# A decoder layer on one core: gates, branch projections and first FFN projection with tokens stationary, results turned over

## The chip, the core and the metric

The kernel runs on one core of a Trainium2 chip. TensorE multiplies a stationary operand, loaded into its array by a weight load, with a moving operand; VectorE and ScalarE do the elementwise work, GpSimd a little, and SyncE's queue (SP) issues the loads. The metric is the device time of one execution in microseconds, the median of several runs. A profile of one execution gives the rows that are shown below; in it PE is TensorE's matmul, PEld its weight load, DVE VectorE, ACT ScalarE, POOL GpSimd and SPq the SyncE queue.

## What is computed

One layer of a hybrid decoder for 256 tokens of width 2048, in float32. Cut to what matters here:

```python
h = modulate(rms_norm(x, norm1_g), sh1, sc1)
u, lru_gate, q, k, v, mix_gates = split(h @ w_in + b_in)
y_lru = rg_lru(causal_depthwise_conv(u)) * gelu(lru_gate)
y_attn = sliding_window_attention(q, k, v, sinks)
gate_lru, gate_attn = split(sigmoid(mix_gates))
merged = gate_lru * (y_lru @ w_lru_out) + gate_attn * (y_attn @ w_attn_out)
x = x + g1 * (merged @ w_o)
h2 = modulate(rms_norm(x, norm2_g), sh2, sc2)
gate, up = split(h2 @ w_ffn_in)
x = x + g2 * ((silu(gate) * up) @ w_ffn_out)
return rms_norm(x, final_g)
```

`w_in` has 22 slabs of 512 columns (the last eight are the mixer gates), each branch projection and `w_o` four, `w_ffn_in` 22 (eleven of gate, eleven of up), and `w_ffn_out` has 44 k-tiles of 2048 columns.

## The kernel before

**Split products.** Every float32 operand is split into a high part (a copy to fp32r by ScalarE, `do_hi`, L285) and a low part (the rest, by VectorE, `do_lo`, L297). A product is three: high x high, high x low, low x high, summed in PSUM (`mm3`, L327 to L329).

**Steps.** The weights come as items of 1024 columns: two k-tiles (128 rows of weights each) of a slab of 512 columns, 512 KB. `step(i)` (L308) issues loads six items ahead, high parts four and low parts three ahead, writes the products of item i into TensorE's order, and then lets other work in. What follows a slab's products (its *post*, a generator) advances by one stage at the start of each later step. Work that belongs to no slab (*sides*: the modulations, the RG-LRU, the attention) advances in stages at the end of a step, as far as a model of the engines' pace, which is part of the program, lets it in. All engines work in the order that this program writes; there is no other scheduler.

**Order of the layer.** The first projection's slabs for u, the GeLU gate, q, k, v (`wi`); the gates of the first branch (`wgl`, 4 slabs); the RG-LRU branch's projection (`wl`, 4); the gates of the second branch (`wga`, 4); the attention's projection (`wa`, 4); `wo` (4); the second norm; then for s in 0 to 10 a gate slab (`fg`) and an up slab (`fu`); the last projection (`pf`, `pl`).

**Three forms of product.** In `add_slab` (L331) the weights are stationary (128 columns of them) and the 256 tokens move: 12 products of 256 columns for a k-tile of a slab, and the result has features along the partitions. With `in_rows` the tokens are stationary (128 of them) and 512 weight columns move: 6 products of 512 columns, and the result has tokens along the partitions. Before, only the V slab (`wi` with SL_V) used `in_rows`. The last projection has a loop of its own with the same shape (L1093). The FFN's first projection uses `add_wide`: weights stationary, and the high and the low part of h2 side by side as 512 moving columns (L1000), then the low part of the weights with 256 columns (L1005): 8 products a k-tile, and two halves that are added afterwards (L1019, L1020). A slab thus has 192 products of 256 columns, or 96 of 512, or 64 of each.

**Posts that the change touches.** `gate_post` (L796): four sigmoids on ScalarE, with the bias as a value for each partition. `lru_post`, `att_post`: two multiplications by the gate on VectorE (L807, L815), the addition of both branches (L817), the split into `mh`, `ml` (L820, L823). `gate_f_post`, `up_f_post`: halves added, SiLU (L1027), multiplied (L1037), split into `fh`, `fl` (L1040, L1043). The results `mh`, `ml`, `fh`, `fl` must have features along the partitions: they are the operands of `wo` and of the last projection.

**PSUM.** Two pools of four banks: `ps_w` (two banks for a slab, so two slabs at a time; `fg` takes all four) and `ps_m` (side work; `fu` takes all four).

## Time and profile before

| | us |
|---|---|
| median of 3 runs (1611.21 to 1613.03) | 1611.26 |
| span of the profiled execution, first to last instruction | 1607.2 |
| TensorE busy | 1591.6 |
| VectorE busy | 1146.6 |
| ScalarE busy | 798.5 |

The profile covers one execution, from its first to its last instruction; the median lies 4.1 us above that span. TensorE's products are pipelined and their ends are modelled: a row's duration is longer than the distance to the next product's start, so rates are read from starts.

### The profile page before, as it was taken

To read this page: it belongs to the slowest core of one execution; us is meant where nothing else is said; L and a number is where in the kernel's file an instruction comes from. 1 tells how busy PE (TensorE), PEld (TensorE's weight loads), DVE (VectorE), ACT (ScalarE), POOL (GpSimd) and SP (SyncE) were. 2 spreads that over 40 slices of the span, in tenths; PEclk is the share of its full clock that TensorE was granted. 3 is DMA by queue.
4 is the path that set the end of the run, shared out by engine and by line. 5 is a ranking of instruction groups with operands and counts; after the bars stand their busy time and mean duration, and the time that the engine had idled before them with its cause. 6 is when DMAs were issued, how large, how long until landed. Compare 5 with 4: busy or idle time off the path is not lost.

```text
span 1607.2 us, 26845 instructions
## 1 busy us (share of the span) xinstructions
PE 1591.6 (99%) x10642; PEld 1460.8 (91%) x10642; DVE 1146.6 (71%) x1472; ACT 798.5 (50%) x1058; POOL 3.0 (0%) x9
## 2 busy tenths in 40 slices
PE   8999999999999999999999999999999999999998
PEld 6999999999999999999998888888888888888886
DVE  6889988989888878788557888455555555444465
ACT  4754444586854455444446444444444444333343
POOL 0000000000000000000000000000000000000000
PEclk9999999999999999999999999999999999999999
DMA  9999998766687878998756898666656566766663
GB/s 319 340 332 327 329 333 285 281 197 226 205 268 247 288 259 273 331 321 298 241 179 226 303 322 314 192 184 185 186 183 194 184 186 207 253 194 195 194 190 127
DMA packets 112596, 397.55 MB, mean 247 GB/s; under 512 B 12499, under 2 KB 13651, under 8 KB 112085
## 3 DMA queue, kind: packets, MB, share of 16 engines
q1 hardware_dynamic: 112470, 395.83, 73.6%
q8 instruction: 83, 1.36, 0.3%
q14 instruction: 43, 0.35, 0.1%
HBM read 391.59 MB, written 4.19 MB: 246 GB/s over the span
## 4 chain that ended last, share of the span: by engine, by line
PE 97%; DVE 1%; DMA 1%; ACT 1%; issue 0%; SPq 0%; ACTq 0%; DVEq 0%
PE pf L1093 11%; PE fu L1000 10%; PE fg L1000 10%; PE wi L329 6%; PE wi L328 6%; PE wi L327 6%; PE fg L1005 5%; PE fu L1005 5%; PE pl L1093 3%; PE wgl L327 2%; PE wo L328 2%; PE wo L327 2%; PE wa L329 2%; PE wa L328 2%; PE wa L327 2%; PE wo L329 2%
## 5 line engine op out<-in xcount | busy, mean ns | idle before, releaser
L285 ACT CAST hi<-raw 128x1024 fp32r<-128x1024 f32 (+1 forms) x552 | 565.0, 1027 | 733.3 <-PE pf L1093 108.0
L297 DVE TENSOR_TENSOR lo<-raw,hi 128x1024 fp32r<-128x1024 f32 (+1 forms) x552 | 655.6, 1192 | 361.8 <-PE pf L1093 92.8
L1000 PE MATMUL fg<-h_both,hi 128*128 128x512 f32 x704 | 250.5, 400 | 0.5 <-DVE h_both L952 0.5
L1000 PE MATMUL fu<-h_both,hi 128*128 128x512 f32 x704 | 249.8, 399 | 0.0
L327 PE MATMUL wi<-h_both,hi 128*128 128x256 f32 x784 | 222.6, 284 | 0.0
L329 PE MATMUL wi<-h_both,lo 128*128 128x256 f32 x784 | 222.1, 283 | 0.5 <-DVE lo L297 0.5
L328 PE MATMUL wi<-h_both,hi 128*128 128x256 f32 x784 | 221.9, 283 | 0.0
L1005 PE MATMUL fu<-h_both,lo 128*128 128x256 f32 x704 | 197.7, 281 | 0.0
L1005 PE MATMUL fg<-h_both,lo 128*128 128x256 f32 x704 | 197.7, 281 | 0.0
L1000 PEld LDWEIGHTS fg<-h_both,hi 128*128 128x128 f32 x704 | 132.3, 188 | 34.2 <-DVE h_both L952 0.7
L1000 PEld LDWEIGHTS fu<-h_both,hi 128*128 128x128 f32 x704 | 132.3, 188 | 33.5 <-ACT pa L588 0.3
L329 PEld LDWEIGHTS wi<-h_both,lo 128*128 128x128 f32 x784 | 150.4, 192 | 0.8 <-DVE lo L297 0.7
L328 PEld LDWEIGHTS wi<-h_both,hi 128*128 128x128 f32 x784 | 150.5, 192 | 0.2
L327 PEld LDWEIGHTS wi<-h_both,hi 128*128 128x128 f32 x784 | 150.4, 192 | 0.2
L1005 PEld LDWEIGHTS fg<-h_both,lo 128*128 128x128 f32 x704 | 133.0, 189 | 0.7 <-issue 0.7
L1005 PEld LDWEIGHTS fu<-h_both,lo 128*128 128x128 f32 x704 | 133.0, 189 | 0.2 <-issue 0.2
L414 DVE CUSTOM_DVE_ANT_0 aw<-aw,crow,modc 128x1024 f32<-128x1024 f32 x79 | 100.8, 1280 | 14.2 <-DMA aw<-in_ada_t_dram 14.0
L414 DVE CUSTOM_DVE_ANT_0 aw<-aw,crow,vec 128x1024 f32<-128x1024 f32 x79 | 100.9, 1280 | 4.9 <-DMA aw<-in_ada_t_dram 4.8
L1093 PE MATMUL pf<-lo,fh 128*128 128x512 f32 x264 | 88.5, 389 | 0.0
L1093 PE MATMUL pf<-hi,fh 128*128 128x512 f32 x264 | 88.4, 389 | 0.0
L1093 PE MATMUL pf<-hi,fl 128*128 128x512 f32 x264 | 88.4, 389 | 0.0
L327 PE MATMUL wl<-yh,hi 128*128 128x256 f32 x256 | 74.9, 293 | 0.0
(228 smaller groups left out, 2930.5 us busy)
## 6 DMA issues: line engine op xcount, KB each, us to landing
raw<-in_w_f_dram SPq DMA_DIRECT2D x176, 512.0 KB, 3.5
raw<-in_w_in_dram SPq DMA_DIRECT2D x160, 512.0 KB, 6.4
aw<-in_ada_t_dram SPq DMA_DIRECT2D x158, 512.0 KB, 5.6
raw<-in_w_f2a_dram SPq DMA_DIRECT2D x44, 512.0 KB, 4.2
raw<-in_w_lru_dram SPq DMA_DIRECT2D x32, 512.0 KB, 6.2
raw<-in_w_att_dram SPq DMA_DIRECT2D x32, 512.0 KB, 6.6
raw<-in_w_o_dram SPq DMA_DIRECT2D x32, 512.0 KB, 3.6
aw<-in_ada_g_dram SPq DMA_DIRECT2D x32, 512.0 KB, 5.2
```

Of the source, the lines that this page charges most:

```text
L285: nc.scalar.copy(hi[:, :cols], live[i][0][:, :cols])
L297: nc.vector.tensor_tensor(lo[:, :cols], raw[:, :cols], f32(hi[:, :cols]), op=ALU.subtract)
L327: nc.tensor.matmul(ps, lhsT=lh, rhs=rh, start=start, stop=False, skip_group_check=True)
L328: nc.tensor.matmul(ps, lhsT=lh, rhs=rl, start=False, stop=False, skip_group_check=True)
L329: nc.tensor.matmul(ps, lhsT=ll, rhs=rh, start=False, stop=stop, skip_group_check=True)
L414: nc.vector.tensor_tensor_reduce(out=r, in0=r, in1=crow[:, j * CH:(j + 1) * CH], op0=ALU.mult, op1=ALU.add, scale=1.0, scalar=dst if j els ...
L1000: nc.tensor.matmul(banks[f].rearrange("p j n -> p (j n)"), lhsT=hi[:, cs], rhs=h2["both"][:, kt, :, :].rearrange("p j n -> p (j n)"), star ...
L1005: nc.tensor.matmul(banks[f][:, 0, :], lhsT=lo[:, cs], rhs=h2["both"][:, kt, 0, :], start=False, stop=kt == NK - 1, skip_group_check=True,)
L1093: nc.tensor.matmul(fin[t, n], lhsT=l[:, rows(t)], rhs=w[:, c0:c0 + 512], start=kt == 0 and k == 0, stop=kt == (EARLY if (t, n) == (1, 3) e ...
```

## The change

The 16 slabs `wgl`, `wl`, `wga`, `wa` now go through `add_slab` with `in_rows`; so do the 22 slabs of the FFN's first projection, and `add_wide` is gone. Their results have tokens along the partitions. For the gates the bias is then a row: it is loaded into every partition (`load_gate_bias`, one load of 128x512 for each gate slab, issued at the slab's third step) and added by VectorE, and one sigmoid follows. The products with the gates stay as they were, on (2, 512) in place of (4, 256). The merged slabs and the FFN's hidden slabs are turned over by TensorE (`turned`: 8 transposes of 128x128 into two banks of `ps_m`), and split out of PSUM (`parts_of`). The attention's mask is made later, in the buffer of `rx`, to make room for the bias buffer.

```diff
+    def in_rows_of(bank):
+        return bank.rearrange("p j n -> p (j n)")
...
-    def add_slab(slab, name, act, k0, k1, post, in_rows=False, before=None):
+    def add_slab(slab, name, act, k0, k1, post, in_rows=False, before=None, late=0):
...
+                if a == k0 + late and before is not None:
+                    before()
                 if a == k0:
-                    if before is not None:
-                        before()
                     banks.extend(wtile(f"{name}_{k0}_{i}") for i in range(2))
...
         free(b4=4)
+        make_mask()
...
+    def load_gate_bias(s):
+        def before():
+            bias[s] = sp.tile([P, 512], F32, tag="bm", name=f"bm{s}", bufs=1)
+            nc.sync.dma_start(bias[s], bm_row[(s - SL_GL) * 512:(s - SL_GL + 1) * 512].partition_broadcast(P))
+        return before
+
     def gate_post(s, i, to):
         def post(banks):
-            dst = b4(f"gate{s}")
-            for f in range(4):
-                b = V_BIN + 4 * s + f
-                nc.scalar.activation(dst[:, f, :], banks[f // 2][:, f % 2, :], AF.Sigmoid, bias=vec[:, b:b + 1])
+            dst, b = b4(f"gate{s}", F32, (2, 512)), bias.pop(s)
+            for t in range(2):
+                nc.vector.tensor_tensor(dst[:, t, :], in_rows_of(banks[t]), b, op=ALU.add)
+            yield 1.4, 0
+            nc.scalar.activation(dst, dst, AF.Sigmoid)
             to[i] = dst
-            yield 0, 1.8
+            yield 0, 1.1
         return post
+
+    def gated(banks, g):
+        for t in range(2):
+            nc.vector.tensor_tensor(g[:, t, :], in_rows_of(banks[t]), g[:, t, :], op=ALU.mult)
...
+    def turned(rows_, name):
+
+        pts = [mtile(f"{name}{i}").rearrange("p (j n) -> p j n", n=S) for i in range(2)]
+        for j in range(4):
+            for t in range(2):
+                nc.tensor.transpose(pts[j // 2][:, j % 2, rows(t)], rows_[:, t, j * P:(j + 1) * P], ident)
+        return pts
+
+    def parts_of(pts, hi, lo):
+
+        for i in range(2):
+            nc.scalar.copy(hi[:, 2 * i:2 * i + 2, :], pts[i])
+        yield 0, 1.2
+        for i in range(2):
+            nc.vector.tensor_tensor(lo[:, 2 * i:2 * i + 2, :], pts[i], f32(hi[:, 2 * i:2 * i + 2, :]), op=ALU.subtract)
+        free(m=2)
+        yield 1.4, 0
 
     def att_post(s):
         def post(banks):
-            for i in range(2):
-                a2 = ga[s][:, 2 * i:2 * i + 2, :]
-                nc.vector.tensor_tensor(a2, banks[i], a2, op=ALU.mult)
-            yield 1.2, 0
+            gated(banks, ga[s])
+            yield 1.4, 0
             nc.vector.tensor_tensor(ga[s], ga[s], gl[s], op=ALU.add)
             yield 1.13, 0
-            mh = b4(f"mh{s}", F32R)
-            nc.scalar.copy(mh, ga[s])
-            yield 0, 0.95
-            ml = b4(f"ml{s}", F32R)
-            nc.vector.tensor_tensor(ml, ga[s], f32(mh), op=ALU.subtract)
+            pts = turned(ga[s], f"mt{s}")
+            yield 0, 0
+            mh, ml = b4(f"mh{s}", F32R), b4(f"ml{s}", F32R)
+            yield from parts_of(pts, mh, ml)
...
-        add_slab(w_lru[s], f"wl{s}", yact, 0, NK, lru_post(s))
+        add_slab(w_lru[s], f"wl{s}", yact, 0, NK, lru_post(s), True)
     for i in range(4):
-        add_slab(w_in[SL_GA + i], f"wga{i}", hact, 0, NK, gate_post(SL_GA + i, i, ga))
+        add_slab(w_in[SL_GA + i], f"wga{i}", hact, 0, NK, gate_post(SL_GA + i, i, ga), True, load_gate_bias(SL_GA + i), 4)
...
     def gate_f_post(s):
         def post(banks):
-            sg = silu[s] = b4(f"sg{s}")
-            yield from halves_added(banks, sg)
-            nc.scalar.activation(sg, sg, AF.Silu)
-            yield 0, 1.1
+            sg = silu[s] = b4(f"sg{s}", F32, (2, 512))
+            for t in range(2):
+                nc.scalar.activation(sg[:, t, :], in_rows_of(banks[t]), AF.Silu)
+            yield 0, 1.3
         return post
 
     def up_f_post(s):
         def post(banks):
             sg = silu.pop(s)
-            up = b4(f"up{s}")
-            yield from halves_added(banks, up)
-            free(m=4)
-            nc.vector.tensor_tensor(sg, up, sg, op=ALU.mult)
-            yield 1.13, 0
...
+            for t in range(2):
+                nc.vector.tensor_tensor(sg[:, t, :], in_rows_of(banks[t]), sg[:, t, :], op=ALU.mult)
+            yield 1.4, 0
+            pts = turned(sg, f"ft{s}_")
+            yield 0, 0
+            fh, fl = b4(f"fh{s}", F32R), b4(f"fl{s}", F32R)
+            yield from parts_of(pts, fh, fl)
...
-        add_wide(w_f1[s], f"fg{s}", True, gate_f_post(s))
-        add_wide(w_f1[11 + s], f"fu{s}", False, up_f_post(s))
+        add_slab(w_f1[s], f"fg{s}", h2act, 0, NK, gate_f_post(s), True)
+        add_slab(w_f1[11 + s], f"fu{s}", h2act, 0, NK, up_f_post(s), True)
```

How the rows of the engines move, at three places (the first name is what is written, behind the arrow what is read, then the size).

TensorE, the first k-tile of the second gate slab (`wgl` is the slab's bank, `h_both` the tokens, `hi` and `lo` the weights' parts), before:

```order
L329 MATMUL wgl_0_0_4561<-h_both,lo_4486 128x256
L327 MATMUL wgl_0_0_4561<-h_both,hi_4443 128x256
L328 MATMUL wgl_0_0_4561<-h_both,hi_4443 128x256
L329 MATMUL wgl_0_0_4561<-h_both,lo_4486 128x256
L327 MATMUL wgl_0_1_4562<-h_both,hi_4443 128x256
L328 MATMUL wgl_0_1_4562<-h_both,hi_4443 128x256
L329 MATMUL wgl_0_1_4562<-h_both,lo_4486 128x256
```

and now:

```order
L320 MATMUL wgl_0_0_4465<-lo_4416,h_both 128x512
L321 MATMUL wgl_0_0_4465<-hi_4385,h_both 128x512
L319 MATMUL wgl_0_1_4466<-hi_4385,h_both 128x512
L320 MATMUL wgl_0_1_4466<-lo_4416,h_both 128x512
L321 MATMUL wgl_0_1_4466<-hi_4385,h_both 128x512
```

The products with a low half of the weights stay in the middle of the k-tile; two rows of 256 columns become one of 512, and a bank now holds 128 tokens in place of 256 features.

VectorE, behind the first gate slab (`uc` is the convolution of the RG-LRU, `lo` the low halves of the weights, `yl` the branch's low part), before:

```order
L297 TENSOR_TENSOR lo_4486<-raw_4370,hi_4443 128x1024
L297 TENSOR_TENSOR lo_4516<-raw_4401,hi_4484 128x1024
...
L645 SCALAR_TENSOR_TENSOR uc_4432<-acc_585,vec,uc_4432 128x255
L297 TENSOR_TENSOR lo_4559<-raw_4441,hi_4514 128x1024
L701 TENSOR_TENSOR yl_4480<-uc_3376,yh_4479 128x1024
L297 TENSOR_TENSOR lo_4598<-raw_4482,hi_4557 128x1024
```

and now:

```order
L286 TENSOR_TENSOR lo_4416<-raw_4336,hi_4385 128x1024
L286 TENSOR_TENSOR lo_4434<-raw_4355,hi_4414 128x1024
...
L638 SCALAR_TENSOR_TENSOR uc_4374<-acc_577,vec,uc_4374 128x255
L812 TENSOR_TENSOR gate_4456<-wgl_0_0_4276,bm_4319 128x512
L812 TENSOR_TENSOR gate_4456<-wgl_0_1_4277,bm_4319 128x512
L286 TENSOR_TENSOR lo_4463<-raw_4383,hi_4432 128x1024
L286 TENSOR_TENSOR lo_4490<-raw_4412,hi_4461 128x1024
L694 TENSOR_TENSOR yl_4410<-uc_3376,yh_4409 128x1024
```

The two additions of the gates' bias stand ahead of the next low half, and the branch's low part moves one low half back.

TensorE, in the second FFN gate slab, where the first hidden slab (`sg`) is turned over (`ft`), now:

```order
L319 MATMUL fg_0_1_8941<-hi_8872,h_both 128x512
L320 MATMUL fg_0_1_8941<-lo_8895,h_both 128x512
L321 MATMUL fg_0_1_8941<-hi_8872,h_both 128x512
L836 MATMUL ft_0_8957<-ident,sg_8762 128x128 x4
L836 MATMUL ft_1_8958<-ident,sg_8762 128x128 x4
L319 MATMUL fg_0_0_8940<-hi_8893,h_both 128x512
```

Before there was nothing but the slab's products at this place; now the transposes stand between its first step and its second.

## Rows read from the trace of the kernel before

**Rows 1.** The page: busy time and share of each engine; the chain's shares.

```profile
PE 1591.6 (99%) x10642; PEld 1460.8 (91%) x10642; DVE 1146.6 (71%) x1472; ACT 798.5 (50%) x1058; POOL 3.0 (0%) x9
...
PE 97%; DVE 1%; DMA 1%; ACT 1%; issue 0%; SPq 0%; ACTq 0%; DVEq 0%
```

**Rows 2.** Waits of TensorE: who waited for whom, us in total, times, longest.

```profile
PE fg L1000 <- DVE h_both L952: 0.5, 1, 0.5
PE wi L329 <- DVE lo L297: 0.5, 1, 0.5
```

**Rows 3.** Timeline of TensorE (start, us, instruction): first products of `wa` and of `wo`.

```profile
667.15 0.28 PE L327 MATMUL wa<-oh,hi 128*128 128x256 f32 x1
...
759.31 0.28 PE L327 MATMUL wo<-mh,hi 128*128 128x256 f32 x1
```

**Rows 4.** Timeline of TensorE: first products of an up slab and the gate slab after it.

```profile
1065.76 0.40 PE L1000 MATMUL fu<-h_both,hi 128*128 128x512 f32 x1
...
1088.37 0.40 PE L1000 MATMUL fg<-h_both,hi 128*128 128x512 f32 x1
```

**Rows 5.** The chain (start, us, what) in the last projection; timeline within the V slab.

```profile
1359.89 179.58 PE pf L1093 x792
...
200.33 0.39 PE L328 MATMUL wi<-lo,h_both 128*128 128x512 f32 x1
...
201.69 0.39 PE L328 MATMUL wi<-lo,h_both 128*128 128x512 f32 x1
```

**Rows 6.** Windows: stretch, its length, each engine's busy us, granted clock, DMA share, GB/s.

```profile
358.00:457.00 99.00, 99.00 (x802) 98.15 (x801) 91.16 (x118) 73.69 (x98) 0.00 (x0) 1.00 0.67 221
457.00:563.50 106.50, 106.50 (x851) 103.19 (x850) 89.08 (x153) 50.18 (x94) 0.00 (x0) 1.00 0.80 270
563.50:667.00 103.50, 103.50 (x824) 100.19 (x823) 81.79 (x127) 52.99 (x85) 0.00 (x0) 1.00 0.82 284
667.00:759.20 92.20, 92.20 (x771) 92.20 (x770) 77.22 (x91) 37.34 (x37) 1.81 (x1) 1.00 0.92 316
...
859.00:1000.00 141.00, 141.00 (x800) 122.21 (x799) 120.40 (x138) 72.68 (x97) 0.00 (x0) 1.00 0.91 315
```

**Rows 7.** Timeline of TensorE around eight transposes; their group (busy us, mean ns).

```profile
521.95 0.28 PE L329 MATMUL wl<-yh,lo 128*128 128x256 f32 x1
522.07 1.04 PE L762 MATMUL pt<-ident,sc 128*128 128x128 f32 x8
522.86 0.36 PE L327 MATMUL wl<-yh,hi 128*128 128x256 f32 x1
523.07 0.29 PE L328 MATMUL wl<-yl,hi 128*128 128x256 f32 x1
...
L762 PE MATMUL pt<-ident,sc 128*128 128x128 f32 x48 | 6.5, 272 | 0.0
```

**Rows 8.** Groups by line and form: busy us, mean ns, idle before, releaser.

```profile
L1020 DVE TENSOR_TENSOR up<-fu,up 128x256 f32<-128x256 f32 x44 | 17.9, 423 | 6.4 <-ACT up L1019 6.4
L1020 DVE TENSOR_TENSOR sg<-fg,sg 128x256 f32<-128x256 f32 x44 | 17.8, 423 | 5.9 <-ACT sg L1019 5.8
L1019 ACT COPY sg<-fg 128x256 f32<-128x256 f32 x44 | 15.7, 372 | 7.8 <-PE fg L1005 7.7
L1019 ACT COPY up<-fu 128x256 f32<-128x256 f32 x44 | 15.6, 372 | 7.2 <-PE fu L1005 7.2
L478 DVE TENSOR_TENSOR acc<-wi,bvb 128x512 f32<-128x512 f32 x2 | 1.3, 683 | 0.0
```

**Rows 9.** Timelines of VectorE and TensorE where the second gate slab begins.

```profile
379.52 2.35 DVE L297 TENSOR_TENSOR lo<-raw,hi 128x1024 fp32r<-128x1024 f32 x2
...
381.01 0.28 PE L327 MATMUL wgl<-h_both,hi 128*128 128x256 f32 x1
```

**Rows 10.** Timeline of VectorE behind the last attention slab.

```profile
759.51 0.69 DVE L815 TENSOR_TENSOR gate<-wa,gate 128x512 f32<-128x512 f32 x1 [0.75 <-PE wa L329]
760.12 1.22 DVE L297 TENSOR_TENSOR lo<-raw,hi 128x1024 fp32r<-128x1024 f32 x1
761.25 1.22 DVE L817 TENSOR_TENSOR gate<-gate,gate 128x1024 f32<-128x1024 f32 x1
```

**Rows 11.** Waits of VectorE for modulations' loads; the bias load (KB, us to landing).

```profile
DVE aw L414 <- DMA aw<-in_ada_t_dram: 18.7, 23, 1.6
...
bvb<-in_bv_row_dram SPq DMA_DIRECT2D x1, 256.0 KB, 7.8
```

More of the change, by code (lines that the diff above doesn't have):

```diff
@@ L190, in hybrid_layer @@
     make_identity(nc, ident)
-    mask = const.tile([P, 256], F32, name="mask")
-    nc.vector.memset(mask, 0.0)
-    nc.gpsimd.affine_select(
-        out=mask[:, 0:P], in_=mask[:, 0:P], compare_op=ALU.is_gt, fill=NEG, base=0,
-        pattern=[[1, P]], channel_multiplier=-1,
-    )
-    nc.gpsimd.affine_select(
-        out=mask[:, P:256], in_=mask[:, P:256], compare_op=ALU.is_ge, fill=NEG, base=0,
-        pattern=[[-1, P]], channel_multiplier=1,
-    )
     clock = {"pe": 0.0, "dve": 0.0, "act": 0.0, "dma": 0.0, "slack": SLACK[0]}
@@ L703, in lru, with make_mask @@
         y_hi[g], y_lo[g] = yh, yl
+    masks = []
+    def make_mask():
+        mask = sp.tile([P, 256], F32, tag="rx", name="mask", bufs=1)
+        masks.append(mask)
+        nc.vector.memset(mask, 0.0)
+        nc.gpsimd.affine_select(
+            out=mask[:, 0:P], in_=mask[:, 0:P], compare_op=ALU.is_gt, fill=NEG, base=0,
+            pattern=[[1, P]], channel_multiplier=-1,
+        )
+        nc.gpsimd.affine_select(
+            out=mask[:, P:256], in_=mask[:, P:256], compare_op=ALU.is_ge, fill=NEG, base=0,
+            pattern=[[-1, P]], channel_multiplier=1,
+        )
     at_hi, at_lo = {}, {}
@@ L717, in attention @@
             per = 512 // nkeys
-            mk = mask[:, 256 - nkeys:]
+            mk = masks[0][:, 256 - nkeys:]
             yield 0, 0, 0, blk + 1
@@ L979, in hybrid_layer, with h2act @@
     f_hi, f_lo, silu = {}, {}, {}
[L981 to L1021 removed]
+    def h2act(kt):
+        return h2["both"][:, kt, 0, :], h2["both"][:, kt, 1, :]
     def gate_f_post(s):
         def post(banks):
[L1025 to L1028 removed]
+            sg = silu[s] = b4(f"sg{s}", F32, (2, 512))
+            for t in range(2):
+                nc.scalar.activation(sg[:, t, :], in_rows_of(banks[t]), AF.Silu)
+            yield 0, 1.3
         return post
@@ L1341, in _layout @@
         "ada_t": a_t, "ada_g": ada_w[:, 5 * D:].reshape(NK, P, D),
-        "w_in": slabs(f("w_in")[0]), "bv_row": f("b_in")[0, 6656:7168], "bg_row": ada_b[None, 5 * D:], "lru_w": lru,
+        "w_in": slabs(f("w_in")[0]), "bv_row": f("b_in")[0, 6656:7168], "bm_row": f("b_in")[0, 7168:], "bg_row": ada_b[None, 5 * D:], "lru_w": lru,
         "w_lru": slabs(f("w_lru_out")[0]), "w_att": slabs(f("w_attn_out")[0]), "w_o": slabs(f("w_o")[0]),
```

58 lines of the change are left out of this document (7 added, 51 removed).

## The prediction

> **What bounds the kernel now.** I read the page's shares and its chain first: TensorE is busy for 1591.6 of 1607.2 us, and 97% of the chain that ended last is TensorE [rows 1]. The waits of TensorE confirm it: after the first 46 us the longest one for another engine is 0.5 us [rows 2]. A busy TensorE is not yet one at its peak, so the second reading is the distance between the starts of neighbouring products. A slab (512 columns of weights, 16 k-tiles) with weights stationary is 192 products of 256 columns: the four attention slabs run from 667.15 to 759.31 us without any side work, 23.04 us a slab, 120.0 ns a product [rows 3]. A slab of the first FFN projection, 64 products of 512 and 64 of 256 columns, takes 1088.37 - 1065.76 = 22.61 us [rows 4]. With tokens stationary and 512 weight columns moving, which the last projection and the V slab already do, one product comes every 179.58 / 792 = 0.2267 us, and in the V slab (1.36 us for six) the same [rows 5]. So 512 columns cost 240.0 ns as two products and 226.7 ns as one: some 13 ns go with each instruction, whatever its width. TensorE's granted clock was 1.00 in all those stretches [rows 6].
>
> **The change, part by part.**
>
> *Products.* 16 slabs (gates and branch projections) go from 192 products at 120.0 ns to 96 at 226.7 ns: 96 x 0.2267 = 21.76 us, 1.28 us less each, 20.4 us in all. The 22 FFN slabs go from 22.61 to the same 21.76 us: 0.85 us each, 18.7 us. All of it is on TensorE, which is the chain, so it counts in full as long as nothing else comes late.
>
> [...]
>
> *Transposes.* Merged slabs (4) and FFN hidden slabs (11) are now turned by TensorE: 15 groups of 8 transposes, 120 in all. The attention has such groups. From the last product before one (521.95) to the second after it (523.07) pass 1.12 us where two products take 0.24, so a group puts in 0.88 us [rows 7]. 15 x 0.88 = 13.2 us on the chain. The bounds: 8 x 0.109 (the pace inside, without the entry and exit) is much the same, 0.87; the row's whole modelled time is 1.04, 15.6 us in all. I take 13.2.
>
> [...] The trace has 272 ns as the duration of one [rows 7], but eight in a row overlap and took 0.88 us together, so the sum goes by the row.
>
> *VectorE and ScalarE, gates and branches.* Each of 8 gate slabs loses four sigmoids on ScalarE from PSUM, gains one over 1024 columns, and gains two bias additions on VectorE like the V slab's, 1.3 us for two [rows 8], 10.4 us in all. VectorE is busy 91.16 + 89.08 + 81.79 + 77.22 = 339.3 of the 401.2 us from 358 to 759.2 [rows 6]. After the change it has 349.7 us of work in 401.2 - 20.4 + 3.5 = 384.3 us, 91% instead of 85%. It fits, but not with the same slack at every place. At the tightest, the low half for the second gate slab is done at 379.52 + 1.22 = 380.74 (the first of two) and TensorE starts on it at 381.01 [rows 9]. VectorE is packed there with the scan's convolution, the order there is unchanged, and TensorE now comes 1.28 us earlier: it waits about 1.0 us. The additions come right behind, and each addition goes ahead of a low half that TensorE needs two steps (5.4 us) later. I put 1.5 us of such waits into the sum; bounds: 0, and 8 x 1.3 = 10.4 us if every gate slab's additions came straight onto the path. Nothing below 0, since no wait for VectorE is there to remove.
>
> *VectorE and ScalarE, FFN.* The eight copies and eight additions of halves for each pair of slabs go (15.7 + 15.6 us ScalarE, 17.8 + 17.9 us VectorE by [rows 8]). VectorE gets room where it was busy 120.4 of 141 us [rows 6]. Off the path: worth nothing, but it is the cover of the next point.
>
> *The new wait.* TensorE's queue is in order, so a transpose that waits for VectorE holds all products behind it. In the FFN it stands a step (2.72 us) after the slab's end; it needs two 512-column products, which, as the attention slabs show, end 759.51 + 0.69 = 0.9 us after the slab's end at 759.31 [rows 10]: 1.8 us to spare. In the merge it stands two steps (5.44 us) behind and needs the addition too, which ended 761.25 + 1.22 = 762.47, 3.2 us after; with one modulation reduction in between (1.28 + 0.08) 4.5 us. 0.9 us are left. I cost it at nothing; a reduction that waits for its load (23 times, 1.6 us at most [rows 11]) would make it 0.7 us, four times.
>
> *Loads and the rest, at nothing.* Eight bias loads of 256 KB join SP's queue; the existing one took 7.8 us to land [rows 11], and each is issued two steps into its slab, 16 us before use. The buffer it waits for was read two steps earlier, so the weight loads behind it are not held. The last modulation reductions stand six steps later in VectorE's order, still 19 steps before the slab that needs them. The mask's one VectorE and two GpSimd instructions move from the start, where they were not on the chain, to the end of h's stages, long before the attention. The FFN's banks move to the other pool, two a slab of four, so one slab is drained while the next fills.
>
> *Sum*, against the profiled span: 1607.2 - 20.4 - 18.7 + 13.2 + 1.5 = 1582.8 us. The median of the runs, 1611.26, lies 4.1 us above that span; with the same 4.1 the forecast is 1586.9, say **1587 us**, 1.5% less.
>
> **Rivals.**
>
> 1. *VectorE lags in the gate and branch stage.* For: 91% busy and one margin of 0.3 us [rows 9]. Against: elsewhere the margins are steps, and every slab end lets VectorE wait for TensorE again. Price: the bound above, 10.4 instead of 1.5: 1582.8 + 8.9 + 4.1 = 1595.8 us.
> 2. *VectorE paces that stage altogether.* Then 401.2 us do not shrink but grow by the 10.4 of additions, and the FFN alone gives 18.7 - 11 x 0.88 = 9.0: 1607.2 + 10.4 - 9.0 + 4.1 = 1612.7 us, no change. Against: it has idle time of 62 us in the stage.
> 3. *The transposes wait, and the kernel gets slower.* The place is TensorE's queue before each of the 15 groups. If VectorE delivers a step late, each costs 2.72 us: 40.8 us, 1586.9 + 40.8 = 1627.7 us. It outweighs the gain (24.4 us) from 1.6 us a group, and is slower beyond 0.2% from 1.8 us. Against: the 1.8 and 0.9 us to spare worked out above.
> 4. *The 512-column product does not keep 226.7 ns in its new places, but takes 240 ns*, as two of 256. Then a slab is 23.04 us: the 16 give nothing, the 22 lose 0.43 each, and the transposes come on top: 1607.2 + 9.5 + 13.2 + 1.5 + 4.1 = 1635.5 us. Against: the V slab has the very same operands [rows 5]. [...]
> 5. *The transposes do not overlap between the wider products.* Each then costs its full duration, 272 ns: 120 x 0.272 = 32.6 us, 1586.9 + 19.4 = 1606.3 us. Against: the 0.88 us of eight [rows 7].
>
> That the change does not do what it says is excluded by the order of the changed program: 512 wide rows stand where the 256 wide stood.
>
> **How the numbers follow.** About 0.2% (3.2 us) is what a measurement can tell from no change. Chances: the forecast 0.80 (its own range 1583 to 1592: no waits and 1.04 us a group as the ends, and the spread of the runs), rival 1 0.10, rival 2 0.03, rival 3 0.03, rival 4 0.02, rival 5 0.02. Faster: 0.80 + 0.10 + 0.02 = 0.92; same 0.03; slower 0.05. The range, 1583 to 1598, takes in the forecast and rival 1.
>
> **What would show it.** Right: an FFN slab of 21.8 us and, with its transposes, 22.7 for each second one; attention slabs of 21.8 + 0.9; products of 512 columns 226.7 ns apart; transposes in 15 groups without idle time before them; about 1 us of TensorE waiting for a low half near 380 us; VectorE about 91% busy from 358 to 743. Wrong: TensorE idle before the transposes (rival 3), waits for low halves that sum to more than 5 us (rivals 1, 2), starts farther apart than 230 ns (rival 4), or groups of over 1.2 us without a wait (rival 5).

## The result, and the profile after

The changed kernel takes **1601.11 us** (median of 7 runs, 1597.50 to 1603.26); the kernel before took 1611.15 us beside it (1603.41 to 1613.03). The ratio is 0.9946, 95% interval 0.9925 to 0.9967: 10 us faster. The forecast was 1586.9 us, 24.4 us faster, and its range ended at 1583 and 1598: some 14 us of the expected gain are missing.

The page of after, busy time and chain, beside [rows 1]:

```profile
PE 1573.8 (98%) x8522; PEld 1359.8 (85%) x8522; DVE 1124.5 (70%) x1426; ACT 768.7 (48%) x973; POOL 4.8 (0%) x9
...
PE 86%; DMA 7%; DVE 4%; issue 2%; ACT 1%; SPq 0%; DVEq 0%; ACTq 0%
```

The chain was 97% TensorE; now 11% of it is transfers and VectorE. So something reaches TensorE from outside, which was not so before. TensorE's waits (who waited for whom, us in total, times, longest) name it, and VectorE's own waits go one step further back; beside [rows 2] and [rows 11]:

```profile
PE mt L836 <- DVE gate L853: 5.2, 4, 2.0
...
PE ft L836 <- DVE sg L1031: 2.1, 3, 1.5
PE wl L320 <- DVE lo L286: 1.8, 2, 1.3
```

```profile
DVE aw L406 <- DMA aw<-in_ada_t_dram: 29.3, 32, 2.5
...
DVE pa L573 <- DMA aw<-in_ada_g_dram: 22.1, 21, 2.4
```

The row like the last one, before:

```profile
DVE pa L580 <- DMA aw<-in_ada_g_dram: 14.6, 18, 2.2
```

TensorE waits before all four merged slabs (`mt`) and before some of the FFN's transposes (`ft`). VectorE waits 29.3 us for the loads of the column modulations where it was 18.7 [rows 11], and 22.1 us for those of the row modulation, in the FFN, where it was 14.6.

The rate of the products is what the forecast took. Timeline of TensorE (start, us, instruction), first products of an up slab, of the gate slab behind it, and of the next up slab:

```profile
1196.41 0.39 PE L319 MATMUL fu<-hi,h_both 128*128 128x512 f32 x1
...
1218.17 0.39 PE L319 MATMUL fg<-hi,h_both 128*128 128x512 f32 x1
...
1240.83 0.39 PE L319 MATMUL fu<-hi,h_both 128*128 128x512 f32 x1
```

A slab is 21.76 us, and 22.65 us with its eight transposes, so a group costs 0.89 us. Before it was 22.61 [rows 4]. What went wrong lies between the slabs. Stage by stage, from first product to first product in the traces (us; "forecast" is the row before less the slabs' gain plus 0.88 a group, without any wait; "x_early" is the last and fastest kernel of the experiments):

| stage | before | forecast | after | x_early |
|---|---|---|---|---|
| first projection | 311.8 | 311.8 | 312.4 | 314.2 |
| two gate and two branch stages, 16 slabs | 401.4 | 383.6 | 392.4 | 385.5 |
| output projection | 92.2 | 93.0 | 94.3 | 93.7 |
| second norm | 7.2 | 7.2 | 6.7 | 6.7 |
| FFN's first projection, 22 slabs | 501.1 | 491.2 | 494.9 | 491.4 |
| last projection, first part | 179.6 | 180.5 | 180.4 | 180.4 |

After lies 8.8 us above the forecast in the gates and branches, 1.3 in the output projection and 3.7 in the FFN. Nearly all of it is idle time of TensorE. The second merge shows how it arises. VectorE and TensorE (start, us, instruction, in brackets the idle time ahead and what ended it):

```profile
705.42 1.22 DVE L286 TENSOR_TENSOR lo<-raw,hi 128x1024 fp32r<-128x1024 f32 x1
709.11 1.28 DVE L406 CUSTOM_DVE_ANT_0 aw<-aw,crow,vec 128x1024 f32<-128x1024 f32 x1 [2.48 <-DMA aw<-in_ada_t_dram]
710.32 0.08 DVE L406 DVE_READ_ACCUMULATOR2_ANT modc<- 128x1 f32 x1
710.32 1.28 DVE L821 TENSOR_TENSOR gate<-wa,gate 128x512 f32<-128x512 f32 x2
711.52 1.22 DVE L286 TENSOR_TENSOR lo<-raw,hi 128x1024 fp32r<-128x1024 f32 x1
712.66 1.22 DVE L853 TENSOR_TENSOR gate<-gate,gate 128x1024 f32<-128x1024 f32 x1
```

```profile
711.68 0.39 PE L321 MATMUL wa<-hi,ol 128*128 128x512 f32 x1
714.02 1.07 PE L836 MATMUL mt<-ident,gate 128*128 128x128 f32 x8 [1.95 <-DVE gate L853]
```

VectorE stands still for 2.48 us before a modulation's reduction whose load has not arrived, and the products for the merge are written behind that reduction. The addition ends at 713.9; without the 2.48 us it would have ended at 711.4, ahead of the end of TensorE's last product before the transposes (711.68 + 0.23). One late load thus becomes 2.1 us of TensorE.

Why the load was late shows in SyncE's queue. The reduction ahead of it on VectorE, the issue of the late load, and the queue's waits in the attention slabs before (first line) and after (second line):

```profile
700.87 1.28 DVE L406 CUSTOM_DVE_ANT_0 aw<-aw,crow,modc 128x1024 f32<-128x1024 f32 x1 [0.98 <-DMA aw<-in_ada_t_dram]
...
702.19 0.33 SPq L377 DMA_DIRECT2D aw<-in_ada_t_dram  x1
```

```profile
SPq L385 <- DVE modc L414: 58.3, 22, 4.5
...
SPq L377 <- DVE modc L406: 67.3, 25, 4.9
```

In these slabs the loads of modulations have two buffers (`N_ADA`), and a load stands in the queue until a reduction frees one: the late load goes out at 702.19, right behind the reduction that ends at 702.15, and VectorE can go on at 709.11. Before it was the same. From issue to landing these loads took 5.5 us (median of the attention slabs), 5.7 before (the weights' loads between them 7.0, before 6.5). So they did not travel longer; they went out too late for the reductions that were asked of them.

Not every wait of TensorE has a late load ahead of it. At 459 and 463 us it waits 2.1 us for low halves, and VectorE has no idle time there: two reductions stand back to back ahead of the second of these low halves.

```profile
458.93 1.28 DVE L406 CUSTOM_DVE_ANT_0 aw<-aw,crow,vec 128x1024 f32<-128x1024 f32 x1
...
460.13 1.28 DVE L406 CUSTOM_DVE_ANT_0 aw<-aw,crow,modc 128x1024 f32<-128x1024 f32 x1
```

Windows of after (stretch, length, busy us of PE, PEld, DVE, ACT, POOL, granted clock, DMA share, GB/s) beside the last two of [rows 6]:

```profile
667.00:759.20 92.20, 88.10 (x413) 73.04 (x412) 77.29 (x97) 35.65 (x38) 0.00 (x0) 1.00 0.94 320
859.00:1000.00 141.00, 138.64 (x618) 113.62 (x617) 113.72 (x118) 66.32 (x79) 0.00 (x0) 1.00 0.93 317
```

The DMA engines were 92% and 91% busy there before, at 316 and 315 GB/s [rows 6]; now 94% and 93%, at 320 and 317. TensorE works through a branch slab in 5.6% less time (21.76 against 23.04 us), and hardly more bytes come. That the engines had no more to give is not shown by this: from 60 to 120 us the same execution moved 344 GB/s.

### The profile page after: what moved, and what is told of

It reads as the page before. It is cut to its first block, busy times and chain, and to the rows that moved or that the text cites. A ratio compares the mean times of both kernels' runs of the same rounds, so it can differ in the third digit from the quotient of the medians.

```text
span 1600.3 us, 22537 instructions
## 1 busy us (share of the span) xinstructions
PE 1573.8 (98%) x8522; PEld 1359.8 (85%) x8522; DVE 1124.5 (70%) x1426; ACT 768.7 (48%) x973; POOL 4.8 (0%) x9
## 4 chain that ended last, share of the span: by engine, by line
PE 86%; DMA 7%; DVE 4%; issue 2%; ACT 1%; SPq 0%; DVEq 0%; ACTq 0%
PE pf L1085 11%; PE wi L321 6%; PE wi L320 6%; PE wi L319 6%; PE fg L319 4%; PE fg L320 4%; PE fg L321 4%; PE fu L320 4%; PE fu L319 4%; PE fu L321 4%; PE pl L1085 3%; DMA aw<-in_ada_g_dram 3%; DMA aw<-in_ada_t_dram 2%; PE wo L319 2%; PE wo L320 2%; PE wo L321 2%
## 5 line engine op out<-in xcount | busy, mean ns | idle before, releaser
L319 PE MATMUL fg<-hi,h_both 128*128 128x512 f32 x352 | 139.5, 396 | 0.0
L320 PE MATMUL fu<-lo,h_both 128*128 128x512 f32 x352 | 137.0, 389 | 0.3 <-DVE lo L286 0.3
L321 PE MATMUL fg<-hi,h_both 128*128 128x512 f32 x352 | 137.1, 390 | 0.0
L320 PE MATMUL fg<-lo,h_both 128*128 128x512 f32 x352 | 137.1, 389 | 0.0
L321 PE MATMUL fu<-hi,h_both 128*128 128x512 f32 x352 | 136.9, 389 | 0.0
L319 PE MATMUL fu<-hi,h_both 128*128 128x512 f32 x352 | 136.9, 389 | 0.0
L406 DVE CUSTOM_DVE_ANT_0 aw<-aw,crow,vec 128x1024 f32<-128x1024 f32 x79 | 100.9, 1279 | 14.6 <-DMA aw<-in_ada_t_dram 14.5
L319 PEld LDWEIGHTS fg<-hi,h_both 128*128 128x128 f32 x352 | 66.1, 188 | 14.4 <-issue 1.0
L320 PEld LDWEIGHTS fu<-lo,h_both 128*128 128x128 f32 x352 | 66.1, 188 | 14.4 <-DVE lo L286 0.7
L320 PEld LDWEIGHTS fg<-lo,h_both 128*128 128x128 f32 x352 | 66.1, 188 | 14.2 <-issue 1.0
```

Of the source, the lines that this page charges most:

```text
L319: nc.tensor.matmul(ps, lhsT=lh, rhs=rh, start=start, stop=False, skip_group_check=True)
L320: nc.tensor.matmul(ps, lhsT=lh, rhs=rl, start=False, stop=False, skip_group_check=True)
L321: nc.tensor.matmul(ps, lhsT=ll, rhs=rh, start=False, stop=stop, skip_group_check=True)
L406: nc.vector.tensor_tensor_reduce(out=r, in0=r, in1=crow[:, j * CH:(j + 1) * CH], op0=ALU.mult, op1=ALU.add, scale=1.0, scalar=dst if j els ...
```

## The experiments

**The theory.** The program's clock counts 2.62 us for a step, whatever its shape. In the gates and branches a real step took 2.88 us before and takes 2.72 now. (In the FFN it took 2.83, an eighth of 22.61.) The loads of modulations and their reductions are let in by that clock, so against real time they are let in 6% faster, 4% in the FFN. The loads do not follow, VectorE stands before its reductions, and what TensorE needs is queued behind. **Rivals:** the transposes themselves (their place in TensorE's queue), VectorE's load of work, a late start through the moved mask or the new input.

**The transposes, later or left out.** In `turn_later` an empty stage stands ahead of the transposes, so TensorE reaches them one step later. In `no_turn` they are left out, and the slabs are split as they lie, not turned over.

```diff
             yield 1.13, 0
+            yield 0, 0
             pts = turned(ga[s], f"mt{s}")
...
             yield 1.4, 0
+            yield 0, 0
             pts = turned(sg, f"ft{s}_")
```

> The changed kernel with the transposes one step later in TensorE's order (an empty stage between the last VectorE product and the turn, in both places). Theory A (TensorE stands in its queue because VectorE's product for the turn is queued behind a modulation reduction that waits for its load): the idle time before the transposes (5.9 us at the four merges, 2.9 us in the FFN) goes to under 1 us, and the median falls by 7 to 9 us against the changed kernel, to some 1593 us. Rival (VectorE has no room there, and the lag only shows at the transposes first): the waits come back as waits for low halves, and the median stays within 2 us of the changed kernel's.

> The changed kernel without the transposes: the merged and the hidden slabs are split as they are, tokens along the partitions, so the products that follow multiply other numbers. It prices the turn: 15 groups at 0.89 us and 8.8 us of waits before them, 22 us less than the changed kernel, some 1579 us, if the turn and its waits are all that the change put on TensorE. If the waits are only VectorE's lag showing there, 13 to 15 us less, some 1587 us.

`turn_later` took 1597.05 us, ratio to the kernel before 0.9913 (0.9895 to 0.9932), so some 5 us under after by the ratios, not 7 to 9. The waits before the `ft` groups are gone, and three of four `mt` groups cost 0.89 us (one 1.05). But one new wait of 2.37 us for a low half came up in the attention slabs, and VectorE's waits for column loads stayed at 26.2 us: the sixteen slabs of gates and branches took 391.8 us beside 392.4 in after. `no_turn` took 1591.29 us, 0.9873 (0.9854 to 0.9893); from the first projection on it is 11.2 us shorter than after, not even the 13.2 us that the transposes take themselves, and it lies above both times that were expected. The waits had moved:

```profile
PE wa L320 <- DVE lo L286: 2.9, 3, 1.6
PE wo L321 <- DVE lo L286: 1.9, 1, 1.9
PE wl L320 <- DVE lo L286: 1.5, 2, 0.9
PE fu L320 <- DVE lo L286: 1.4, 2, 1.2
```

```profile
DVE aw L406 <- DMA aw<-in_ada_t_dram: 29.4, 36, 2.6
...
DVE pa L573 <- DMA aw<-in_ada_g_dram: 18.4, 20, 2.4
```

With no transposes at all VectorE waits for column loads as long as in after (29.4 us), and TensorE meets the delay at the low halves. The transposes were where the delay surfaced, not its cause.

**Reductions only when the load is well in.** `loads_here` lets a reduction in four model-us later.

```diff
-LATE = 1.0
+LATE = -3.0
```

> The changed kernel with a modulation reduction let into VectorE's order only when its load should, by the program's own pace, have arrived 3 us before (LATE -3.0 for 1.0). Theory A (the loads are what VectorE waits for ahead of the turn): VectorE's waits for modulation loads, about 29 us in all in the changed kernel, fall below 10 us, TensorE's idle time before the four merges' transposes falls from 5.9 to under 2 us, and the median falls by 4 to 7 us; the reductions end later, but before the last slab of w_o. Rival (VectorE's own work is what is late): its waits for loads fall, TensorE's waits and the median stay within 2 us.

All groups of transposes cost 0.89 us and the attention slabs 89.72 us, without any wait. In the sixteen slabs of gates and branches VectorE waited for no load at all (25.1 us in after), and they took 384.6 us. Yet the kernel took 1633.23 us, 1.0137 (1.0116 to 1.0157): the first projection became 10 us longer, and the reductions that had been put off had to be finished in one piece ahead of the last output slab.

```profile
PE wo L321 <- DVE lo L286: 30.7, 2, 29.9
```

So the waits in question go with the reductions, but putting these off without a plan costs more than it gives.

**The clock set right.** `paced` counts a step of the changed slabs as 0.945 of a step (2.72 / 2.88); `paced_later` adds the empty stage of `turn_later`.

```diff
+RATE = 0.945
...
-                False, 1,
+                False, RATE if in_rows and name[:2] != "wi" else 1,
```

> The changed kernel with one number of the program's pace put right: a step of a slab with tokens stationary counts as 0.945 of a step (2.72 / 2.88 us), so the modulations' loads and reductions are let in at the same rate per microsecond as in the kernel before. Theory C (the steps got shorter, the program's clock did not know it, so it asked for more bytes per microsecond than the DMA moved, VectorE waited for the loads, and TensorE for VectorE): VectorE's waits for modulation loads fall from 29.5 to about the 19 us of before, TensorE's waits for VectorE (some 11 us) fall to under 4 us, the median falls by 6 to 9 us against the changed kernel, to 1592 to 1595 us. Rival (VectorE's own work and its order is what is late, whatever the loads do): waits and median stay within 2 us of the changed kernel's 1601.

> The same with the transposes one step later as well. Theory C: the waits left are those for low halves; 7 to 10 us under the changed kernel, 1591 to 1594 us, and no more than 3 us under the paced one. If the in-order wait ahead of the transposes is a cause of its own, it is more than 3 us under the paced one.

`paced` took 1596.66 us, 0.9922 (0.9898 to 0.9946); `paced_later` 1592.09 us, 0.9901 (0.9879 to 0.9923). `paced` is thus some 4 us under after by the ratios, where 6 to 9 were expected. VectorE's waits for column loads fell to 19.9 and 21.3 us, about the 18.7 of before. The waits in the FFN are gone in both (VectorE's for row loads 22.1 us in after, 2.3 and 2.2 here), `paced` keeps one wait of 1.3 us at a merge. In `paced_later` the sixteen slabs take 385.0 us with no wait of TensorE over 0.25 us, and one of 2.2 us remains in the second output slab; it is taken up below. `paced_later` lies 4.6 us under `paced`, more than the 3 that were to tell whether the place of the transposes is a cause of its own; but the intervals overlap, and in the profiles the branch slabs and the output stage differ by 1.7 us together, so this stays open. Two things keep this from being the old pace and nothing else. In the FFN 0.945 is slower than the old pace (2.72 / 2.83 is 0.96), and the row waits lie far under the 14.6 us of before. And 13 of the 75 column reductions leave the sixteen slabs for the output projection, so VectorE also has less to do there.

**The loads made light.** `light_loads` transfers half of each modulation load and reduces that half twice: VectorE has no less work (357.4 us busy in the sixteen slabs, 339.9 in after), half the modulations' sums are left out.

```diff
-                nc.sync.dma_start(t, self.srcs[self.n])
+                nc.sync.dma_start(t[:, :CH // 2], self.srcs[self.n][:, :CH // 2])
```

> The changed kernel in which each load of modulation weights brings half its columns, and VectorE reduces that half twice in place of the two halves once: the modulations are other numbers, VectorE's time is the same or a few per cent more, the bytes of these loads are halved (48 MB fewer in all). Theory C: VectorE's waits for these loads go under 5 us, TensorE's waits for VectorE under 3 us, and the median falls by 7 to 10 us, to some 1592 us. Rival (VectorE is too full): TensorE's waits stay at 9 us or more, and the median stays or rises.

1591.90 us, 0.9898 (0.9876 to 0.9921), some 8 us under after by the ratios, with more work on VectorE.

```profile
DVE pa L578 <- DMA aw<-in_ada_g_dram: 12.0, 11, 2.4
DVE aw L407 <- DMA aw<-in_ada_t_dram: 9.1, 8, 2.9
```

The waits for loads shrink from 51 to 21 us, not to under 5: a load of half the size is still late 19 times. These loads too go out only behind a reduction (26 in the attention slabs, where the DMA engines were busy 79% at 255 GB/s), so full DMA engines do not explain them. TensorE keeps 1.8 us of waits at the merges and the 1.7 us at the start of the first branch projection; the sixteen slabs took 389.2 us, the FFN 491.4. What more buffers for these loads would do was not run.

**The old kernel with the new fault.** `before_fast` is the kernel before with the clock counting 1.058 of a step in the same stages; nothing of the change is in it.

```diff
+RATE = 1.058
...
-                False, 1,
+                False, RATE if name[:2] in ("wg", "wl", "wa") else 1,
```

> The kernel before with one number changed: in the steps of the gates, branch projections and first FFN projection the program's clock now counts 1.058 of a step (the ratio of a real step before, 2.88 us, to one after, 2.72 us). The products, and all work of the layer, stay as they were; only the modulations' loads and reductions are let in earlier. Theory (loads asked for faster than they arrive, waited for in VectorE's in-order queue): the old kernel gets the waits of the new one. VectorE waits for the modulations' column loads 25 us or more in all instead of 17 to 19, TensorE waits for low halves in the branch stages 3 to 8 us in all, the median becomes 1614 to 1619 us. Rival (the waits belong to the new transposes and additions alone): TensorE's waits stay under 1 us, the median within 1 us of the kernel before, 1610.5 to 1612.5.

It took 1618.17 us beside 1612.63, 1.0039 (1.0020 to 1.0058): slower, as the theory wanted. Waits of TensorE and of VectorE:

```profile
PE fg L1006 <- DVE lo L298: 2.5, 3, 1.2
...
PE wgl L330 <- DVE lo L298: 1.3, 2, 0.8
PE wa L330 <- DVE lo L298: 1.2, 2, 0.9
...
PE fu L1006 <- DVE lo L298: 0.9, 1, 0.9
```

```profile
DVE aw L415 <- DMA aw<-in_ada_t_dram: 23.3, 26, 2.5
...
DVE pa L581 <- DMA aw<-in_ada_g_dram: 14.3, 15, 1.7
```

The 5.9 us of TensorE's waits for low halves are in none of the rows of before [rows 2]. The column waits, 23.3 us, stayed a little under the 25 expected, and the gates and branches have 2.5 us of the 5.9, where 3 to 8 were expected. The other 3.4 us lie in the FFN, where 1.058 is more than the change does (1.04), and VectorE's waits for row loads did not grow there (14.3 us, 14.6 before). So the pace is shown as a cause, alone, without a transpose or a wide product; that it always works through longer waits for loads is not.

**One half of the change.** `ffn_only` leaves gates and branches as before.

```diff
-        add_slab(w_lru[s], f"wl{s}", yact, 0, NK, lru_post(s), True)
+        add_slab(w_lru[s], f"wl{s}", yact, 0, NK, lru_post(s))
...
-        add_slab(w_att[s], f"wa{s}", aact, 0, NK, att_post(s), True)
+        add_slab(w_att[s], f"wa{s}", aact, 0, NK, att_post(s))
```

> The change in the first FFN projection alone; gates and branch projections, and the merge, as before, and no bias row among the inputs. By the sizes read so far the slabs give 22 x 0.85 = 18.7 us and the eleven groups of transposes take 9.8, so the median is 1602.5 us less nothing else; theory (late loads): with the reductions of the second half still let in too fast in the FFN, 2 to 4 us of waits come back, 1604 to 1606.5, and the gates and branches show no wait of over 0.5 us. Rival (each transposed group waits by itself): 11 groups with a wait each, above 1609. The second quarter of x is used at 8.0 us as in the kernel before if the new input shifted it, at 8.7 if the later mask did.

1606.58 us, 0.9963 (0.9949 to 0.9978): 6 us of the 9 that the sizes give. Its profile is of the slowest of ten executions (1614.26 us). There the FFN has two groups of 8 transposes with waits (1.73 and 0.59 us before the first transpose) and lasts 496.6 us, 5 above the 491.4 without waits where 2 to 4 were expected. Another expectation missed: the unchanged attention stage showed a wait of 1.61 us for a low half, and VectorE's column waits were 29.0 us. Delivery thus varies between executions at one and the same order, and the old order has little to spare as well. The second quarter of x was used at 8.85 us.

**What remained: x's reload.** `paced_later` has one wait left. TensorE there, VectorE's wait that goes with it, and the windows around:

```profile
783.68 0.28 PE L321 MATMUL wo<-ml,hi 128*128 128x256 f32 x1
786.19 0.58 PE L322 MATMUL wo<-mh,lo 128*128 128x256 f32 x1 [2.24 <-DVE lo L287]
786.57 0.41 PE L320 MATMUL wo<-mh,hi 128*128 128x256 f32 x1
786.78 0.41 PE L321 MATMUL wo<-ml,hi 128*128 128x256 f32 x1
```

```profile
DVE x1T L906 <- DMA x1T<-in_x_t_dram: 3.7, 1, 3.7
```

```profile
783.00:786.10 3.10, 0.95 (x8) 0.75 (x7) 3.10 (x5) 1.41 (x2) 0.00 (x0) 0.96 0.88 274
786.10:789.50 3.40, 3.31 (x16) 3.31 (x17) 3.40 (x5) 0.69 (x1) 0.00 (x0) 0.54 0.99 302
789.50:793.00 3.50, 3.50 (x31) 3.50 (x30) 3.29 (x5) 2.10 (x2) 0.00 (x0) 1.00 1.05 372
```

The slower pace carries the last reductions into the output projection, where all of x (2 MB) is loaded again at once. VectorE waits 3.7 us for its first tile, then 1.8 us for a modulation, and TensorE 2.2 us for VectorE. Two attempts followed: `best`, with 0.965 in place of 0.945, which ends the reductions sooner, and `best_row`, the same with the gates' bias taken from the row that brings the values' bias (no additional input).

> The whole change, with the products that turn a slab over written one stage later and a step of those slabs counted as 0.965 of a step by the program's clock (0.945 before): the last column reduction then stands five steps ahead of the first output slab's end instead of at its sixth step. Theory: no wait of over 1.5 us at the output projection, no stretch at half clock, 1588 to 1591 us against 1592.1 for 0.945. Rival (the loads are late at any rate near this, the waits only move): a wait of 2 us or more in the branch or output stages and 1592 to 1596 us.

> The same, with the gates' bias read from the row that already brings the values' bias, so that the program has as many inputs as the kernel before. If the additional input shifts the first loads, the second quarter of x is used at 8.0 us instead of 8.5 to 9.3 and the first product of the first projection's steady stage comes about 1 to 2 us earlier: 1587 to 1590 us. If not: 8.5 or more, and the same time as the kernel with the additional input within 1 us.

Neither came out below the kernel with 0.945: 1598.33 us, 0.9916 (0.9893 to 0.9938), and 1599.07 us, 0.9918 (0.9893 to 0.9944). The reductions still met x's reload (VectorE's wait for x 3.4 us in both, low-half waits up to 2.9 us in the output projection). The wait for row loads was back at 20.0 and 17.8 us. `best_row` used the second quarter of x at 8.99 us, so leaving the new input out did not bring the first loads forward. Then x itself: `x_early` (0.945 again) loads its tiles one at a time, each about a slab ahead.

```diff
-                x1T.extend(load_x("x1T"))
...
+            if s < 3:
+                load_x1(s + 1)
...
-        add_slab(w_o[s], f"wo{s}", mact, 0, NK, o_post(s), before=x_first if s == 3 else None)
+        add_slab(w_o[s], f"wo{s}", mact, 0, NK, o_post(s), before=x_first if s == 3 else (lambda: load_x1(0)) if s == 0 else None,
+                 late=8 if s == 0 else 0)
```

> As the paced kernel with later transposes (0.945), but the four tiles of x that the output projection needs again are loaded one at a time, the first four steps into the middle of the first output slab and each other one a slab ahead of its use, instead of all four (2 MB) at once right ahead of the first use. Theory (after pacing, what is left of the lost time is x's reload queued behind the last modulations): the 3.4 to 3.7 us wait of VectorE for x and TensorE's 2.4 us wait in the second output slab go, with the half clock behind it; first output slab to second norm 93 us instead of 96.8; median 3 to 4 us under the same kernel without this edit on this chip. Rival (the low halves there wait for the reductions, whatever x does): a wait of 1.5 us or more stays and the two are within 1 us.

> The paced kernel with later transposes once more, beside the changed kernel on one chip. If 0.965 was the worse rate, this gives 1591 to 1593 us as before, 9 us under the changed kernel. If the other chip made the difference, it gives 1592 to 1598 here and its distance to the changed kernel is what counts.

> The changed kernel once more, in another execution, on the chip of the two paced kernels. Theory (loads let in too fast): waits of TensorE again before all or most merged groups and at two or three FFN groups, 9 to 14 us in all, VectorE's waits for column loads 25 to 32 us, median 1600 to 1602 us. If those waits were an accident of the one execution: under 5 us and below 1596.

On one chip, beside 1611.53 us for the kernel before: `x_early` 1589.36 us, 0.9861 (0.9844 to 0.9877); `paced_later_2` 1591.40 us, 0.9875 (0.9860 to 0.9890); `after_2` 1602.68 us, 0.9938 (0.9915 to 0.9961). `paced_later_2` lies 11.3 us under `after_2`: the pace and the empty stage, on one chip. In `x_early` the wait for x is gone, and so is TensorE's wait of 2.2 us behind it, which `paced_later_2` still has. TensorE's waits for a low half, the second of them in the output projection:

```profile
PE wi L322 <- DVE lo L287: 2.3, 2, 1.5
...
PE wo L322 <- DVE lo L287: 0.4, 1, 0.4
```

The output projection took 93.7 us where `paced_later_2` took 95.5 and the first run of that kernel 96.8. The stretch at half clock is no part of this pair: `paced_later_2` had the wait and kept a granted clock of 1.00. The medians differ by 2.0 us, not by the 3 to 4 expected, and their intervals overlap: the mechanism is shown in the trace, its worth in the median only roughly. `after_2` had the waits of after again: 5.6 us before the four merges, 31.9 us of VectorE for column loads; only those in the FFN were nearly gone. So the merges' waits came in both profiles of this kernel (5.2 and 5.6 us), the FFN's varied. Whether 0.965 fell behind by its pace or by its chip stays open, since 0.965 was not run beside 0.945.

**The start.** `before_again` is the kernel before once more; `before_mask_late` is the kernel before with the mask made late alone, as in the change.

```diff
         free(b4=4)
+        make_mask()
```

> The kernel before, once more, for a second profile. Theory A (the start of a run varies by itself): the first product of the first projection starts anywhere from 46 to 51 us in this kernel too, and the rest of the span, from there to the end, is 1561 us within 1 us. Theory B (the change made the start slower): 46 us within 0.5 us again.

> The kernel before with the change's other edit alone: the attention's mask is made late, in the buffer of rx. Theory B (this edit, by moving what lies at the start or where the buffers lie, makes the start slower): the first product of the first projection starts 2 to 4 us later than the 46 to 47 us of before, and the second quarter of x is there at 8.6 us or later in place of 7.5 to 8.0. Theory A (the start differs by itself): as before, and the median is within 2 us of before's.

1612.78 us for the first, 1608.18 us and 0.9991 (0.9974 to 1.0008) for the second (3.5 us under the kernel before beside it, where within 2 was expected): the mask's place costs nothing that the medians show. The first projection's steady part began at 46.1 us in the profile of before, at 47.3 here, at 48.9 in `before_fast` and at 49.7 with the late mask; after-like kernels lie between 47.3 and 50.8. The second quarter of x was used at 7.54 us here and at 8.03 with the late mask, as in before. The profile of before was an early starter of a spread of some 4 us. With one profile of each kernel, what sets that spread stays open; the late mask and the new input are not shown to. From the first projection to the end `before_again` took 1559.0 us, not 1561 within 1: its FFN was 1.6 us shorter.

## Why the prediction missed

**Right.** The rate: 226.7 ns a product in the new places, slab 21.76 us, so 1.28 and 0.85 us less a slab. The 13 ns that were to go with each instruction, "whatever its width", are an estimate from two widths, 2 x 120.0 - 226.7 ns; the streams of before and after show these two, 256 and 512 columns, and for another width it is not shown. The transposes: 0.89 us a group wherever nothing waits, forecast 0.88; rivals 4 and 5 are out. VectorE does not pace the sixteen slabs: 339.9 us busy of their 392.4 us, 87% (forecast 91%), so rival 2 is out. The mask, the bias loads and the FFN's banks: no wait of TensorE is seen to go back to them. Where pace and reload are mended, the stages of `x_early` come to 385.5 and 491.4 us, against 383.6 and 491.2 in the table: apart from the waits the sum of the parts was sound.

**The step that failed** is "The new wait". It named the mechanism, a reduction that waits for its load ahead of the product for the transposes, gave it 0.7 us four times, and costed it at nothing. Measured in after: the four merge groups cost 1.80, 3.04, 2.54 and 2.13 us in place of 0.89, so 6.0 us, and two FFN groups 1.53 and 3.13 us, 2.9 us more. With the low halves the gaps in TensorE's starts come to some 12.5 us, 1.0 of it in the unchanged first projection, where the sum had 1.5. Two things were mis-sized. The delay itself: the longest wait for a load was taken from before (1.6 us), though the change makes TensorE pass the same loads in less time; after had 32 such waits, the longest 2.5 us. And the cover: the FFN was given 1.8 us to spare, "as the attention slabs show", with no reduction counted in, although the row loads of the last modulation are reduced there.

**The step that was not made** lies behind it. The description of the kernel names the pace model ("a model of the engines' pace, which is part of the program"); the prediction does not come back to it. It read the order of the reductions, six steps later, as harmless, and not their time, nor that their loads go out only when a reduction has freed a buffer. `before_fast` shows what was overlooked in the pace.

**The wait that was put at 380 us** (1.0 us before the second gate slab) did not come: in after that slab starts at 385.0, and TensorE loses 0.1 us there (products 0.33 us apart at 385.6 in place of 0.23). The margin of 0.3 us was read to the slab's first product, at 381.01, which takes a high half [rows 9]; the low half is first used at 381.25:

```profile
381.25 0.28 PE L329 MATMUL wgl<-h_both,lo 128*128 128x256 f32 x1
```

So 0.5 us were to spare, and in after VectorE reaches this low half 0.8 us earlier too, counted from the first gate slab's start. That 2.1 us of low-half waits did come in this stage, at 459 and 463 us, close to the 1.5 of the sum, is luck: another place and another reason.

**Around the span.** The 4.1 us between span and median were carried over as a constant. In the runs of this case an execution takes 1.7 to 2.2 us more than its span, once 3.0 (after: 1602.11 and 1600.3). The profiled execution of before was thus, as an estimate from these, one of about 1609 us, some 2 below the median, with an early start. Against the profiled after the account closes: 12.9 us less gain between the first projection and the end, 4.7 later start, 2.3 less around the span, together 15.3; 1602.1 - 1586.9 is 15.2.

**Rival 1** had the engine, the stage and nearly the size: the sixteen slabs lie 8.8 us above the forecast, and the rival put 8.9 us on it. Its reason was VectorE's own work, the additions of the bias. `light_loads` speaks against that: more work on VectorE, and 3.2 us less than after in these slabs. But the crowded queue at 459 us is of this kind, and `paced`, which takes reductions out of the stage, does not separate less work there from loads that are in time.

**Rival 3** had the right place, TensorE's queue before each group, and the wrong price: not 2.72 us at all 15, but 0.6 to 2.2 at six of them. The 8.9 us are over a third of the expected gain and did not turn the sign.

## What to carry to other kernels

A kernel that admits side work by a model of time carries the old step's length in that model. When a step gets shorter, look for everything that is let in by it, and compare how often it asks for a load with how long a buffer takes to come round: freed by a reduction, issued, landed (5.5 us later here), reduced. And in an in-order queue the time to spare is to be counted with the longest wait of each instruction ahead, not with its busy time (in after a reduction of 1.28 us stood 2.48 us for its load); here the empty stage, the pace and the spread of x's reload together brought 0.9946 to 0.9861.

## What the runs showed of the hardware

After some single waits TensorE's granted clock was near half. In `paced_later`, after a wait of 2.4 us (by its starts), the granted clock was 0.54 from 786.1 to 789.5 us and the products behind the wait 0.21 us apart in place of 0.12; as an estimate from these, 0.46 of 3.4 us, that is worth some 1.5 us on top of the wait. The length of the wait does not decide it. `paced_later_2` had the same wait at the same place and stayed at 1.00. `after_2` fell to 0.58 behind a wait of 2.0 us, before its first merge, and not behind one of 2.9 us, before its third (first and second line; the third is `paced_later_2`):

```profile
690.10:694.20 4.10, 4.10 (x16) 3.44 (x17) 3.38 (x4) 2.02 (x3) 0.00 (x0) 0.58 0.73 234
737.00:744.00 7.00, 4.26 (x24) 3.37 (x22) 5.91 (x7) 2.78 (x4) 0.00 (x0) 1.00 0.99 341
...
787.00:790.50 3.50, 3.42 (x28) 3.42 (x29) 3.50 (x7) 0.43 (x1) 0.00 (x0) 1.00 0.95 295
```

What decides it is open. In `loads_here` the granted clock was 0.50 when the wait of 30 us ended, at 864.6, and until 868; from 870 it was 1.00 again.

The FFN's pair of one product of 512 and one of 256 columns, in the kernel before, ran in two rhythms: 353.3 ns a pair in the profile of before (22.61 us a slab), 346.7 ns in the first four slabs of `before_again` (22.19 us). A slab of before was no constant, then: in those four slabs the 0.85 us gained in each would have been 0.4 less.
